# A sliding-window attention layer on one core: a new order of the seven products over three named banks, slots of their own for small tasks, softmax by groups with the sink as a 129th column

## The chip, the core and the metric

The kernel runs on one of the eight cores of a Trainium2 chip. The metric is device time in microseconds, from the program's start to its end. Three runs of the kernel before took 1522.75 to 1527.77 us, with a median of 1525.52. A further execution was taken with the hardware profiler; all busy times, waits and durations below are from that one.

The engines are TensorE (PE; its weight loads are PEld), VectorE (DVE), ScalarE (ACT), GpSimd (POOL) and SyncE (SP), which here only issues DMAs. TensorE writes to PSUM, which has eight banks of 128 x 512 float32.

## The reference

One decoder layer, of a width of 1024, on 4096 tokens: RMSNorm, a combined projection to queries, keys, values and a gate, attention over a window of 128 keys with a T5 bias and a learned sink per head, the gate, the output projection, the residual and a last RMSNorm.

```python
def swa_sink_mixer(xn, w_in, sinks, w_out, t5_table):
    q, k, v, z = jnp.split(xn @ w_in, [nq, nq + nkv, nq + 2 * nkv], axis=-1)
    o = banded_attention(q_heads(q, B, T), kv_heads(k, B, T), kv_heads(v, B, T),
                         t5_table, SWA_WINDOW, sinks)
    return (merge_heads(o, B, T) * jax.nn.silu(z)) @ w_out
...
    s = jnp.where(valid, s + bias[None, :, :, None], NEG)
    sk = jnp.broadcast_to(sinks.astype(jnp.float32).reshape(1, G, R, 1, 1, 1), s.shape[:-1] + (1,))
    p = jax.nn.softmax(jnp.concatenate([s, sk], axis=-1), axis=-1)[..., :-1]
    o = jnp.einsum('bgrnqk,bgnkd->bgrnqd', p.astype(v.dtype), vb)
...
    x = x + y.astype(x.dtype)
    return rms_norm(x, final_g)
```

There are 16 heads of 64 and 4 key-value heads. The sink takes part in the softmax's sum and then falls away.

## The kernel before

The tokens are worked on in 16 blocks of 256 (`tb`). Every float32 operand is held as two float16 halves, high and low, and each matmul is done as three passes (`PASSES`): high by high, high by low, low by high. ScalarE writes the high half and VectorE the low half (a subtraction), which is what the many "split" steps do.

The three large projections (q, z and the output o) are 1024 x 1024 matrices. From the third or fourth block on each is computed by Strassen's scheme in Winograd's form: both sides are cut into 2 x 2 pieces, seven products are formed from pieces and from sums of pieces (`s1`..`s4` on one side, `t1`..`t4` on the other), and the results are added. The first blocks use the plain eight products (`PLAIN`). The sums of the weights are prepared once, during blocks 1 to 3 (`sums`, four steps a matrix); the sums of the activations are made in each block: `x_sum` (GpSimd, in place in the tile `xf`, then the split `xs`) and `split_y` (GpSimd, in place in the tiles `y`, then the split `yo`).

For q and z a product is 48 matmuls of 128 x 128 x 128 (`product_t`, L307); for o it is 12 matmuls of 128 x 128 x 512 (`product_o`, L576). The seven products accumulate in three PSUM banks, which `ORDER` calls X, Z and W: X takes four of them, Z two, W one. After each product its bank is copied (`copy_m`, L336), added (`add_m`, L341; `add_mm` on GpSimd, L346) or passed on. The tag `pj` has three buffers for these banks and for those of the keys and values.

Six of the seven weight pieces of q stay in SBUF (`wq`); the seventh, and all pieces of z and o, are streamed from DRAM, 1 MB each, through a ring of three buffers `ws` (`load_s`, L286). SyncE issues these loads, and in the same queue those of `x` in two layouts (`load_x`: `xin` by rows, L99, and `xf` transposed, L102), of the residual `r` (L554), and the stores (L607). The `xf` halves have one buffer each, so a new half is loaded when the old one's last sum is split.

Attention is done in four pairs a block (a group pair `gp` and a half `t` of the block), each with two groups `e`:

- `scores` (L459): four tiles `s`, one for each of `e` and `r`, in a ring of two banks.
- `post` (L469 to L478): VectorE joins two parts of the score tile and writes score plus bias to the tile `c` (8 rows of 128 columns) with the row's maximum as an accumulated result.
- `exps` (L484 to L494): for all eight rows of the pair VectorE takes the larger of the maximum and the sink, scales it by -1/SCORE (`nm`) and forms the sink's difference (`dd`); ScalarE computes eight exponentials with their sums and one for the sink.
- `normalise` (L499 to L504): VectorE adds the two sums and takes the reciprocal; ScalarE multiplies all eight rows.
- `turn` (L512 to L518): four transposes a group, then the split `pt` and its masked copy `pm`.
- `values` and `gate` (L536, L543): the value products, and `y` = result times the gate `z`.

The order comes from a list of slots, 25 a block. Tasks are entered by `at` into one of four lists of a slot (`first`, `before`, `main`, `after`) and are emitted slot by slot. Block `tb`'s keys and values are in its slots 7 to 10, z in 11 to 17, the pairs from 11 to 39, and its output products in 43 to 49, which are slots 18 to 24 of the next block. A task such as `x_sum` or `split_y` does everything in its one slot: GpSimd's sum, ScalarE's half and VectorE's half. After emission a scheduler orders each engine's instructions by this priority and by when operands are ready, so an engine's order is near to the emitted one but not the same.

## Time and profile before

| | us |
|---|---|
| median of three runs | 1525.52 |
| profiled execution | 1529.2 |
| its span, from the first to the last instruction | 1527.3 |
| 11 steady block periods (430.5 to 1406) | 975.5 |
| mean granted TensorE clock over the span | 0.968 |

Busy time counts the union of an engine's instructions. The granted clock is the share of full speed that TensorE was given; in this trace it is either 1.0 or 0.5 at any moment, so a mean of 0.98 in a stretch means that 4% of it ran at half speed. In the rows of groups, "busy, mean ns" are the group's busy time in us and the mean duration of one instruction; where instructions of a group overlap, busy time over count is less than that mean. "x12" is a count. "[3.03 <-DMA ws<-wost]" is idle time of the engine just before the row, and what ended it.

Over the whole program the queue of SyncE moved 319 GB/s in the first 60 us and 225 GB/s from 430.5 to 1406.

### The profile page before, as it was taken

How to read it: one execution, taken by the hardware profiler on the slowest of the kernel's cores; microseconds unless marked ns; L12 is line 12 of the kernel's file. 1: busy time of each engine (PE TensorE's matmuls, PEld its weight loads, DVE VectorE, ACT ScalarE, POOL GpSimd, SP SyncE). 2: the span in 40 equal slices, each digit the busy share in tenths (PEclk: the TensorE clock that was granted, in tenths of full speed). 3: DMA queues.
4: the chain of work that ended last, by engine and by line, in shares of the span. 5: the costliest groups of instructions: out<-in, count | busy, mean ns of one | idle time of the engine just before them, and what ended most of it. 6: DMA issues, size and time to landing. Idle time of an engine off the chain costs nothing.

```text
span 1527.3 us, 39610 instructions
## 1 busy us (share of the span) xinstructions
PE 1398.7 (92%) x16234; PEld 1096.6 (72%) x16234; DVE 1060.1 (69%) x2783; ACT 955.9 (63%) x2633; POOL 389.1 (25%) x338
## 2 busy tenths in 40 slices
PE   5988899688999998999999898999989899999996
PEld 5987578367587785958778595877859587785952
DVE  8478766848848576776857677685767758676684
ACT  7367676645755676566567556656755665675672
POOL 0002423226204122131413213141321314132133
PEclk9999999799999999999999999999999999999998
DMA  9965654776967657475765747476574757656384
GB/s 367 289 223 173 263 214 179 248 272 254 342 225 252 246 197 280 157 280 166 262 238 201 278 155 276 167 266 238 205 256 160 271 183 251 235 205 251 122 301 185
DMA packets 70662, 356.24 MB, mean 233 GB/s; under 512 B 8752, under 2 KB 10832, under 8 KB 40656
## 3 DMA queue, kind: packets, MB, share of 16 engines
q1 hardware_dynamic: 61952, 336.92, 61.3%
q10 hardware_dynamic: 8528, 16.78, 3.0%
q8 instruction: 127, 2.08, 0.5%
q14 instruction: 55, 0.45, 0.1%
HBM read 318.03 MB, written 35.65 MB: 232 GB/s over the span
## 4 chain that ended last, share of the span: by engine, by line
PE 39%; DVE 27%; ACT 18%; DMA 9%; issue 4%; POOL 2%; SPq 0%; ACTq 0%; POOLq 0%; DVEq 0%
PE pj L307 21%; PE pj L576 11%; ACT c L492 7%; ACT c L504 5%; DVE xs L271 4%; DMA ws<-wost 3%; DVE q L355 3%; DVE pm L518 3%; DVE c L478 2%; PE tp L512 2%; DVE xb L259 2%; DVE pt L515 2%; PE o L536 2%; DVE z L405 2%; DVE xf L251 2%
## 5 line engine op out<-in xcount | busy, mean ns | idle before, releaser
L576 PE MATMUL pj<-ws,yo 128*128 128x512 f16 x1380 | 339.0, 398 | 42.3 <-DMA ws<-wost 14.5
L307 PEld LDWEIGHTS <-ws 128*128 128x128 f16 x6192 | 358.2, 99 | 15.2 <-issue 10.5
L307 PEld LDWEIGHTS <-wq 128*128 128x128 f16 x4800 | 280.4, 99 | 21.9 <-issue 11.8
L492 ACT ACTIVATE c<-c,nm 128x128 f32<-128x128 f32 x512 | 198.1, 388 | 148.0 <-DVE nm L486 146.7
L576 PEld LDWEIGHTS <-yo 128*128 128x128 f16 x1380 | 135.5, 102 | 209.8 <-issue 44.3
L307 PE MATMUL pj<-xb,ws 128*128 128x128 f16 x3024 | 184.0, 223 | 5.3 <-DMA ws<-wzs 3.5
L307 PE MATMUL pj<-xs,ws 128*128 128x128 f16 x3168 | 187.5, 219 | 1.3 <-ACT mc L336 1.3
L307 PE MATMUL pj<-xb,wq 128*128 128x128 f16 x2784 | 179.5, 222 | 8.4 <-ACT xb L258 3.5
L504 ACT ACTIVATE c<-c,rl 128x128 f32<-128x128 f32 x512 | 156.3, 388 | 3.7 <-DVE rl L501 3.7
L336 ACT ACTIVATE mc<-pj 128x512 f32<-128x512 f32 x160 | 93.8, 587 | 90.6 <-PE pj L307 76.3
L459 PE MATMUL s<-K,q 128*128 128x192 f16 x1024 | 111.5, 249 | 17.7 <-DVE m L478 12.4
L515 DVE SCALAR_TENSOR_TENSOR pt<-tp,pt 128x512 f16<-128x512 f32 x128 | 86.5, 680 | 52.8 <-ACT pt L514 52.5
L307 PE MATMUL pj<-xs,wq 128*128 128x128 f16 x2016 | 119.7, 219 | 0.0
L591 POOL TENSOR_TENSOR r<-r,mc 128x512 f32<-128x512 f32 x52 | 70.5, 1366 | 187.1 <-ACT mc L336 185.8
L478 DVE CUSTOM_DVE_ANT_0 c<-s,bias 128x128 f32<-128x128 f32 x496 | 116.1, 282 | 2.5 <-PE tp L512 1.6
L459 PEld LDWEIGHTS <-q 128*128 128x128 f16 x1024 | 84.2, 99 | 36.3 <-DVE m L478 19.0
L268 POOL TENSOR_TENSOR xf<-xf 128x512 f32<-128x512 f32 x56 | 78.3, 1400 | 101.1 <-DVE xb L259 78.1
L518 DVE TENSOR_TENSOR pm<-pt,own_m 128x1024 f16<-128x1024 f16 x128 | 101.5, 796 | 1.4
L514 ACT ACTIVATE pt<-tp 128x512 f16<-128x512 f32 x128 | 74.5, 587 | 42.4 <-PE tp L512 42.0
L156 POOL TENSOR_TENSOR wst<-wst 128x512 f32<-128x512 f32 x48 | 70.0, 1468 | 110.6 <-ACT wst L191 60.5
L326 PE MATMUL pj<-xb,wkv 128*128 128x256 f16 x768 | 92.7, 275 | 4.0 <-ACT xb L258 3.3
L492 ACT ACTIVATION_READ_ACCUMULATOR c<-c,nm 128x1 f32 x512 | 95.7, 187 | 0.0
(98 smaller groups left out, 2098.4 us busy)
## 6 DMA issues: line engine op xcount, KB each, us to landing
ws<-wos SPq DMA_DIRECT2D x63, 1024.0 KB, 6.4
ws<-wzss SPq DMA_DIRECT2D x52, 1024.0 KB, 5.7
ws<-wost SPq DMA_DIRECT2D x52, 1024.0 KB, 5.8
ws<-wzs SPq DMA_DIRECT2D x47, 1024.0 KB, 4.9
xin<-in_x SPq DMA_DIRECT2D x32, 512.0 KB, 5.8
xf<-in_xt SPq DMA_DIRECT2D x32, 512.0 KB, 6.2
r<-in_x SPq DMA_DIRECT2D x32, 512.0 KB, 4.3
out<-r SPq DMA_DIRECT2D x32, 512.0 KB, 5.7
```

The costliest lines, as they stand in the source:

```text
L268: nc.gpsimd.tensor_tensor(s, b[l], b[r], op=OP.subtract)
L307: nc.tensor.matmul(place(p, c), left(kc, wi)[:, c * P:(c + 1) * P], right_x(tb, right, kc, xi), start=fresh and c == 0 and k == 0, stop=c ...
L326: nc.tensor.matmul(p[:, gp * TB:(gp + 1) * TB], wkv[:, kc, wi, gp * P:(gp + 1) * P], xx(tb, xi, kc), start=k == 0, stop=k == 23)
L336: nc.scalar.activation(m, p, AF.Copy, scale=scale)
L459: nc.tensor.matmul(s[:, hp, 0:3 * HD], lhs, rhs, start=hl == 0, stop=hl == 1)
L478: nc.vector.tensor_tensor_reduce(out=cu, in0=sv, in1=b, scale=1.0, scalar=-3e38, op0=OP.add, op1=OP.max, accum_out=self.m[:, u:u + 1])
L492: nc.scalar.activation(cu, cu, AF.Exp, bias=nm[:, u:u + 1], scale=1.0 / SCORE, accum_out=l[:, u:u + 1])
L504: nc.scalar.activation(cu, cu, AF.Copy, scale=rl[:, u:u + 1])
L514: nc.scalar.activation(w[:, 0], p, AF.Copy, scale=SP)
L515: nc.vector.scalar_tensor_tensor(w[:, 1], p, SP, w[:, 0], op0=OP.mult, op1=OP.subtract)
L518: nc.vector.tensor_tensor(self.pm[e].rearrange("p l (h q) -> p (l h) q", h=4), w.rearrange("p l (h q) -> p (l h) q", h=4), own_m[:, None, ...
L576: nc.tensor.matmul(p, YO[left][:, yi, c * P:(c + 1) * P], right(c, wi), start=fresh and k == 0, stop=k == 11, skip_group_check=not fresh)
```

## The change

The matmuls are the same. What changes:

- **Order of the seven products.** Products are no longer in consecutive slots. In a block's output projection they are at slots 43, 44, 46, 48, 49, 47, 52: the sixth (the second on bank Z) comes ahead of the fourth and fifth, and slots between them are left to z and to the next q. The three banks have names of their own, `pa`, `pb`, `pc`, one buffer each, and each chain is told which of them is its X, Z and W.
- **Small tasks in slots of their own.** What a step did in one slot is cut up: `x_sum` (GpSimd) and `x_sum_split`; `sum_y` and `split_y`; `evac_v`, `diff_v` and `split_dv`; `evac_k` by halves; `x_norm` into `x_square` and `x_factor`; GpSimd's additions after a bank's copy. A slot now has eight lists (`PHASES`), and a table (`STEADY`, with `FIRST` and `LAST` for the ends) gives each task its slot. The steps of the weight sums are at slots 13, 17, 21 and 25, not 10, 13, 16 and 19.
- **Softmax.** The score tile `c` has a 129th column that GpSimd fills with the sink. `post` writes the negated, scaled score and reduces by minimum, starting from the sink, so that its accumulated result is the bias of the exponential; the sink's exponential is the 129th column's and is in the row's sum. `exps` and `normalise` are done for a group of four rows at a time. Of the four, ScalarE multiplies two and VectorE two.

```diff
     def x_sum(tb, n):
...
-        s = b[dst]
-        nc.gpsimd.tensor_tensor(s, b[l], b[r], op=OP.subtract)
+        dst, l, r = (x_blk(tb, *b) for b in SUM[n])
+        nc.gpsimd.tensor_tensor(dst, l, r, op=OP.subtract)
+
+    def x_sum_split(tb, n):
+        s = x_blk(tb, *SUM[n][0])
...
+        def post(self, e):
+            g = 2 * self.gp + e
+            if not self.c:
+                self.c = atile([P, 8, P + 1], F32, "c", 2)
...
+                nc.gpsimd.tensor_copy(self.c[:, :, P], sk)
...
-                nc.vector.tensor_tensor_reduce(out=cu, in0=sv, in1=b, scale=1.0, scalar=-3e38, op0=OP.add,
-                                               op1=OP.max, accum_out=self.m[:, u:u + 1])
+                    nc.vector.tensor_tensor_reduce(out=cu, in0=sv, in1=b, scale=-1.0 / SCORE,
+                                                   scalar=sink[:, g, r, hp:hp + 1], op0=OP.add, op1=OP.min,
+                                                   accum_out=self.m[:, u:u + 1])
...
-            nc.vector.tensor_tensor(mx, self.m, sk, op=OP.max)
-            nc.vector.tensor_scalar(nm, mx, -1.0 / SCORE, None, op0=OP.mult)
-            nc.vector.tensor_tensor(dd, sk, mx, op=OP.subtract)
...
+        def exps(self, e):
+            for u in range(4 * e, 4 * e + 4):
+                cu = self.c[:, u, :]
+                nc.scalar.activation(cu, cu, AF.Exp, bias=self.m[:, u:u + 1], scale=-1.0,
+                                     accum_out=self.l[:, u:u + 1])
+
+        def normalise(self, e):
+            rl = work.tile([P, 4], F32, tag="rl", name="rl", bufs=3)
+            nc.vector.reciprocal(rl, self.l[:, 4 * e:4 * e + 4])
+            for u in range(4):
+                cu = self.c[:, 4 * e + u, :P]
+                if u % 2:
+                    nc.scalar.activation(cu, cu, AF.Copy, scale=rl[:, u:u + 1])
+                else:
+                    nc.vector.tensor_scalar(cu, cu, rl[:, u:u + 1], None, op0=OP.mult)
...
+    PHASES = ("bank", "attn", "sum", "split", "soft", "load", "main", "scores")
+    work_of = [{n: [] for n in PHASES} for _ in range(total)]
+
+    def bank(key, name):
+        banks[key] = ps(f"p{name}")
+        return banks[key]
...
-    PLAN = {"q": range(0, 7), "k": 7, "v": 9, "z": range(11, 18), "pairs": (11, 17, 23, 29), "out": range(43, 50)}
+    STEADY = {
+        "q": (0, 1, 3, 5, 6, 4, 9), "k": (7, 8), "v": (10, 12), "z": (11, 13, 14, 15, 17, 16, 20),
+        "o": (43, 44, 46, 48, 49, 47, 52),
...
+        "ysum": {"s1": 40, "s2": 43, "s4": 44, "s3": 46},
+        "ysplit": {"11": 40, "s1": 41, "12": 43, "s2": 44, "s4": 45, "s3": 47, "22": 49},
...
+        "xsum": {"t1": 17, "t2": 23, "t3": 25, "t4": 26}, "xsumsplit": {"t1": 22, "t2": 24, "t3": 26, "t4": 28},
+    }
...
-        at(before, SLOTS + (10, 13, 16, 19)[c], sums, w_q, c, True, sum_q)
+        at("soft", SLOTS + (13, 17, 21, 25)[c], sums, w_q, c, True, sum_q)
```

Two places show how the order moves, both in a steady block, where the output products of one block run beside the sums of x for the next. First SyncE's queue there before; `wos` and `wost` are weights of o, `wzs` and `wzss` of z, and the numbers are buffers:

```order
L286 DMA ws_10062<-wzs22_90 128x4096
L286 DMA ws_10163<-wos11_102 128x4096
L286 DMA ws_10219<-wost1_98 128x4096
L286 DMA ws_10292<-wost2_104 128x4096
L102 DMA xf_11133<-in_xt 128x1024
L286 DMA ws_10357<-wos21_105 128x4096
L102 DMA xf_11135<-in_xt 128x1024
L286 DMA ws_10444<-wost3_103 128x4096
L286 DMA ws_10478<-wos22_99 128x4096
L286 DMA ws_10537<-wost4_101 128x4096
```

And the same queue in the changed kernel, where L302 is `load_s`, L105 `load_xf` and L99 `load_xin`:

```order
L302 DMA ws_11357<-wos11_102 128x4096
L99 DMA xin_16557<-in_x 128x1024
L302 DMA ws_11420<-wost1_98 128x4096
L99 DMA xin_16557<-in_x 128x1024
L302 DMA ws_11482<-wzs22_96 128x4096
L302 DMA ws_11543<-wost2_103 128x4096
L105 DMA xf_12228<-in_xt 128x1024
L302 DMA ws_11619<-wos22_104 128x4096
L302 DMA ws_11646<-wos21_105 128x4096
L105 DMA xf_12230<-in_xt 128x1024
L302 DMA ws_11684<-wost3_100 128x4096
L302 DMA ws_11827<-wost4_99 128x4096
```

The last z weight has moved in among the weights of o, `wos22` ahead of `wos21`, and one more weight stands between the two `xf` loads; the second `xf` load is still just ahead of `wost3`.

Second, VectorE's queue. Before, from the split of the second `xf` half (`xb`) to the split of its last sum (`xs`), and what follows:

```order
L259 TENSOR_TENSOR xb_11923<-xf_11135,xb_11923 128x4x256
L405 SCALAR_TENSOR_TENSOR z_11835<-z_11835,cc_11833 128x512
L515 SCALAR_TENSOR_TENSOR pt0_11901<-tp_11896,pt0_11901 128x512
L405 SCALAR_TENSOR_TENSOR z_11772<-z_11772,cc_11770 128x512
L515 SCALAR_TENSOR_TENSOR pt1_11944<-tp_11939,pt1_11944 128x512
L405 SCALAR_TENSOR_TENSOR z_11920<-z_11920,pj_11405 128x512
L518 TENSOR_TENSOR pm0_11904<-pt0_11901,own_m_110 128x1024
L271 TENSOR_TENSOR xs_12099<-xf_11135,xs_12099 128x4x128
L469 COPY_PREDICATED s_11974<-sel_115,s_11974 128x2x64
L518 TENSOR_TENSOR pm1_11947<-pt1_11944,own_m_110 128x1024
```

In the changed kernel the end of that way, from the last score reduction of the next softmax (`ISA`, on `c`) to the same split (`xs` from `xf_10786`, L287):

```order
L515 ISA m_11813 128x1
L528 RECIPROCAL rl_11863<-l_11607 128x4
L528 RECIPROCAL rl_11971<-l_11607 128x4
L430 SCALAR_TENSOR_TENSOR z_11744<-z_11744,pb_11137 128x512
L534 TENSOR_SCALAR c_11605<-c_11605,rl_11863 128x128 x2
L534 TENSOR_SCALAR c_11605<-c_11605,rl_11971 128x128
L573 SCALAR_TENSOR_TENSOR y00_11893<-o_11843,z_11535 128x512
L534 TENSOR_SCALAR c_11605<-c_11605,rl_11971 128x128
L287 TENSOR_TENSOR xs_12077<-xf_10786,xs_12077 128x4x128
L506 COPY_PREDICATED s_11806<-sel_115,s_11806 128x2x64
```

Before, six operations stand between `xb` and that `xs`. In the changed kernel `xb` (not shown) is 44 rows ahead of it: score reductions, two other splits of sums, `yo`, `pt`, `pm` and the four normalisations come in between.

More of the change, by code (lines that the diff above doesn't have):

```diff
@@ L634, in go, with chain @@
+    def chain(slots, key, names, f, steps):
         def go(n):
-            b = ORDER[n][1]
-            if n in (0, 1, 3):
-                banks[key, b] = ps("pj", 3)
-            f(n, banks[key, b])
+            b = "XZW".index(ORDER[n][1])
+            p = bank((key, b), names[b]) if n in (0, 1, 3) else banks[key, b]
+            f(n, p)
         for n, s in enumerate(slots):
-            at(main, s, go, n)
-            at(before, s + 1, lambda n=n: steps[n](banks[key, ORDER[n][1]]))
-    def chain_t(slots, tb, key, left, place, done):
+            at("main", s, go, n)
+            at("bank", s + 1, lambda n=n: steps[n](banks[key, "XZW".index(ORDER[n][1])]))
@@ L662, in go @@
                 if k == 1:
-                    banks[key, b] = ps("pj", 3)
+                    bank((key, b), names[b])
                 f(i, j, k, banks[key, b], k == 1)
             for k in (1, 2):
-                at(main, slots[2 * b + k - 1], go, k)
-            at(before, slots[2 * b + 1] + 1, lambda b=b, i=i, j=j: done(i - 1, j - 1, banks[key, b]))
-    def plain_t(slots, tb, key, left, place, done):
-        plain(slots, (key, tb),
+                at("main", slots[2 * b + k - 1], go, k)
@@ L671, in plain_t @@
+            at("bank", slots[2 * b + 1] + 1, lambda b=b, i=i, j=j: done(i - 1, j - 1, banks[key, b]))
+    def plain_t(slots, tb, key, names, left, place, done):
+        plain(slots, (key, tb), names,
               lambda i, j, k, p, fresh: product_t(tb, left(f"{i}{k}"), f"{k}{j}", p, place, fresh),
               lambda gp, t, p: done(tb, gp, t, p))
[L675 to L676 removed]
@@ L711, in tile_swa_block @@
-            at(first, s + 10, pr.values)
-            at(first, s + 10, pr.gate)
-        out0 = s0 + plan["out"][0]
-        slots = range(out0, out0 + 7)
-        if tb < PLAIN["o"]:
-            for n, b in enumerate(("11", "21", "12", "22") * 2):
-                at(before, out0 + n - 3, load_s, ("o", n), b, wos[b])
-            for b, s in zip(BLOCKS, (-2, -1, 2, 3)):
-                at(before, out0 + s, split_y, tb, b)
-            plain(slots, ("o", tb),
+            for e, (sc, po, ex, no, tu) in enumerate(((sc0, po0, ex0, no0, tu0), (sc1, po1, ex1, no1, tu1))):
+                at("scores", sc, pr.scores, e)
+                at("attn", po, pr.post, e)
+                at("soft", ex, pr.exps, e)
+                at("soft", no, pr.normalise, e)
+                at("attn", tu, pr.turn, e)
@@ L721, in tile_swa_block @@
+            at("attn", va, pr.values)
+            at("attn", ga, pr.gate)
+        if isplain["o"]:
+            slots = S["oplain"]
+            for n, (b, s) in enumerate(zip(("11", "21", "12", "22") * 2, slots)):
+                at("load", s - 4, load_s, ("o", n), b, wos[b])
+            for b, s in S["yplain"].items():
+                at("split", s, split_y, tb, b)
+            plain(slots, ("o", tb), "cbac" if tb + 1 < PLAIN["z"] else "cabc",
                   lambda i, j, k, p, fresh: product_o(f"{i}{k}", stream(("o", 4 * i + 2 * j + k - 7), f"{k}{j}"), p,
@@ L732, in tile_swa_block @@
-            chain(slots, ("o", tb),
-                  lambda n, p: product_o(LEFT[n], stream("o", RIGHT[n]), p, n in (0, 1, 3)), steps)
-        at(before, out0 - 3, load_r, tb)
+            for n, s in enumerate(S["o"]):
+                at("load", s - 4, load_s, "o", RIGHT[n], wos[RIGHT[n]])
+            for n, s in S["ysum"].items():
+                at("sum", s, sum_y, tb, n)
+            for n, s in S["ysplit"].items():
+                at("split", s, split_y, tb, n)
+            keep = {}
@@ L751, in tile_swa_block @@
+            if tb + 1 >= min(PLAIN["q"], PLAIN["z"]):
+                for n in SUM:
+                    at("sum", S["xsum"][n], x_sum, tb + 1, n)
+                    at("split", S["xsumsplit"][n], x_sum_split, tb + 1, n)
+    for tb in range(NTB):
+        block(tb)
     for t in range(2):
-        x_norm(0, t)
+        x_square(0, t)
+    x_factor(0)
     x_row(0)
```

326 lines of the change are left out of this document (165 added, 161 removed), and 8 rows, old and new, of the table STEADY.

## The prediction

> **What bounds the kernel now.** I read the busy line of the page first, then the stretches, then the timeline of TensorE in one block, the DMA issues of SyncE, and the chain of waits. The busy line says which engine to watch:
>
> ```profile
> PE 1398.7 (92%) x16234; PEld 1096.6 (72%) x16234; DVE 1060.1 (69%) x2783; ACT 955.9 (63%) x2633; POOL 389.1 (25%) x338
> ```
>
> TensorE works for 1398.7 of 1527.3 us, and the change leaves its matmuls as they are: the same 128x128 products, scores, transposes and value products, in another order. So time can only come out of TensorE's idle time and out of time that it works at half clock. The stretches tell where those are (columns: length, then busy time of PE, PEld, DVE, ACT and POOL, then the granted clock and the share of DMA):
>
> ```profile
> 60.00:430.50 370.50, 319.74 (x3595) 248.82 (x3592) 265.43 (x692) 235.69 (x641) 103.35 (x80) 0.94 0.69 250
> 430.50:1406.00 975.50, 927.51 (x11002) 732.88 (x10999) 677.03 (x1808) 610.79 (x1717) 253.34 (x221) 0.98 0.63 225
> 1406.00:1527.30 121.30, 107.04 (x1042) 73.98 (x1040) 74.39 (x207) 69.95 (x214) 28.20 (x24) 0.95 0.55 204
> 695.60:785.10 89.50, 84.51 (x999) 66.50 (x999) 62.04 (x167) 56.32 (x161) 22.86 (x20) 0.98 0.64 226
> 1231.90:1318.20 86.30, 82.70 (x1001) 66.13 (x1000) 61.28 (x165) 55.51 (x159) 22.94 (x20) 1.00 0.66 234
> ```
>
> After the ramp (to 60, not shown) come the early blocks, which also prepare weights (to 430.5), 11 steady blocks, and the end. A steady block takes 975.5 / 11 = 88.7 us, with (975.5 - 927.5) / 11 = 4.4 us of TensorE idle. The last two rows are one block each, with the same 1000 matmuls: at full clock TensorE works 82.7 us on it, at a mean of 0.98 about 84.4. So what a steady block can give at most is 4.4 + (927.5 / 11 - 82.7) = 4.4 + 1.6 = 6.0 us, 66 us in all 11. Where it is lost, TensorE's timeline of one block shows (start, length, and in brackets the idle time before and what ended it):
>
> ```profile
> 757.63 0.40 PE L536 MATMUL o<-pm,dv 128*64 128x512 f16 x1
> 758.78 0.81 PE L536 MATMUL o<-pm,dv 128*64 128x512 f16 x5 [0.74 <-DVE pm L518]
> 760.34 0.93 PE L459 MATMUL s<-K,q 128*128 128x192 f16 x8 [0.75 <-DVE m L478]
> 761.43 2.75 PE L576 MATMUL pj<-ws,yo 128*128 128x512 f16 x12 [0.16 <-DMA ws<-wos]
> 764.01 0.82 PE L459 MATMUL s<-K,q 128*128 128x192 f16 x8
> 767.87 4.44 PE L576 MATMUL pj<-ws,yo 128*128 128x512 f16 x12 [3.03 <-DMA ws<-wost]
> ```
>
> Two waits of 0.75 us for VectorE and one of 3.03 us for a streamed weight. The product after that wait takes 4.44 us in place of 2.75: the half clock. SyncE's issues of the same stretch (the second row of weights, `ws<-wost`, is the one waited for):
>
> ```profile
> 753.66 0.38 SPq L286 DMA_DIRECT2D ws<-wos  x1
> 757.96 0.33 SPq L102 DMA_DIRECT2D xf<-in_xt  x1
> 758.38 0.38 SPq L286 DMA_DIRECT2D ws<-wost  x1
> ```
>
> And the chain of waits, followed back from the late product:
>
> ```profile
> 754.96 1.30 DVE pm L518
> 756.25 1.67 DVE xs L271
> 757.93 0.22 DVE s L469
> 758.15 0.14 SPq L102
> ...
> 758.38 9.35 DMA ws<-wost
> ```
>
> SyncE issues in order. The load of the next `xf` half waits until VectorE has split the last sum of the old one (`xs`, done at 757.9), and the weight queued behind it goes out at 758.4 and lands 9.35 us later. So the weight wait is itself a VectorE wait: the bound beside TensorE is VectorE's queue in the part of a block where the output products run.
>
> **The change part by part, in a steady block.** *Output products among other products.* TensorE now has a z product and parts of two q products between the seven output products. I count what lies between the last `xs` split and the product of the late weight (`wost3`) in the two orders. Before, TensorE has one output product, scores and values left when the split is done at 757.9, 4.6 us of work without the waits. In the new order the split stands where two output products (2 x 2.6), six of the value matmuls (0.7), scores (0.7) and 17 matmuls of a q product (1.0) are still ahead of it: 7.6 us. The page's landing time for these weights is the median of this row, and the worst here is the 9.35 us above:
>
> ```profile
> ws<-wost SPq DMA_DIRECT2D x52, 1024.0 KB, 5.8
> ```
>
> 7.6 against 5.8: I put the weight wait at nothing, with a bound of 9.35 - 7.6 = 1.8 us a block. With the 3 us gap gone the half clock should go too: the block 1231.9 to 1318.2 above kept full clock although TensorE waited there before the same product, only for 1.78 us:
>
> ```profile
> 1302.66 2.75 PE L576 MATMUL pj<-ws,yo 128*128 128x512 f16 x12 [1.78 <-ACT c L504]
> ```
>
> *VectorE's queue.* From the split of the first sum (`xs_11786`) to the last of the four normalisations of the next softmax (`c_11605`), the new order has on VectorE 3 sum splits, 1 `xb`, 3 gates `z` (2 from `cc`, 1 from a bank), 5 predicated copies, 10 score reductions, 2 `yo`, 2 `pt`, 2 `pm`, 1 K copy, 2 reciprocals, 4 normalisations and 1 `y`. What each costs:
>
> ```profile
> L478 DVE CUSTOM_DVE_ANT_0 c<-s,bias 128x128 f32<-128x128 f32 x344 | 80.2, 282 | 0.5
> L518 DVE TENSOR_TENSOR pm<-pt,own_m 128x1024 f16<-128x1024 f16 x86 | 66.7, 776 | 1.1
> L570 DVE TENSOR_TENSOR yo<-y,yo 128x512 f16<-128x512 f32 x78 | 60.2, 771 | 7.6 <-ACT yo L569 6.3
> L515 DVE SCALAR_TENSOR_TENSOR pt<-tp,pt 128x512 f16<-128x512 f32 x86 | 58.4, 679 | 48.9 <-ACT pt L514 48.8
> L271 DVE TENSOR_TENSOR xs<-xf,xs 128x512 f16<-128x512 f32 x44 | 58.2, 1323 | 15.8 <-ACT xs L270 15.8
> L469 DVE COPY_PREDICATED s<-sel,s 128x128 f32<-128x128 int32 x172 | 45.6, 286 | 4.1 <-PE s L459 3.4
> L259 DVE TENSOR_TENSOR xb<-xf,xb 128x1024 f16<-128x1024 f32 x22 | 36.3, 1649 | 0.0
> L405 DVE SCALAR_TENSOR_TENSOR z<-z,cc 128x512 f32<-128x512 f32 x33 | 27.6, 837 | 0.0
> L486 DVE TENSOR_SCALAR nm<-mx 128x8 f32<-128x8 f32 x43 | 7.2, 168 | 1.1
> L476 DVE TENSOR_TENSOR c<-s,bias 128x128 f32<-128x128 f32 x16 | 3.9, 282 | 0.1
> ```
>
> By busy time over count (they overlap a little): 3 x 1.32 + 1.65 + 2 x 0.84 + 0.67 + 5 x 0.265 + 10 x 0.233 + 2 x 0.77 + 2 x 0.68 + 2 x 0.78 + 0.4 + 2 x 0.2 + 4 x 0.2 + 0.69 = 18.4 us. (The z gate from a bank, `y`, the K copy and the reciprocals are estimates by their neighbours: 0.67 and 0.69 like `pt`, 0.4 for half of `pm`, 0.2 like `nm`.) VectorE starts that list when TensorE has 1.2 us left of a z product, since two operations (0.69 and 0.84) stand between. From there to the transposes that need the four normalised pieces TensorE has, beside those 1.2 us, three output products (2.6 each, 761.43 to 764.01 above), one z product, 28 score matmuls, 8 transposes and 12 value matmuls (0.40 and 0.81 for 6 above). The other lengths are in the chain of waits of another block:
>
> ```profile
> 1318.25 8.15 PE pj L307 x144
> 1326.40 0.66 PE s L459 x8
> 1327.06 0.44 PE tp L512 x4
> ```
>
> Three products take 8.15, so 2.7 each, eight score matmuls 0.66 and four transposes 0.44: 1.2 + 7.8 + 2.7 + 2.3 + 0.9 + 1.2 = 16.1 us. VectorE is 2.3 us longer, so **TensorE waits 2.3 us a block**, at the scores whose two banks VectorE must clear and at the value products.
>
> *What I priced by bounds.* A normalisation on VectorE (128x128, SBUF to SBUF) isn't in the trace: it lies between 0.168 (`nm`, 128x8) and 0.282 us (`c` at L476, 128x128 from a bank), and I take 0.2, near the smaller, as those rows overlap to 0.24 and 0.17. The reduction now takes its start value from `sink`, a column in place of a constant. It may cost nothing, and at most what a column adds elsewhere:
>
> ```profile
> L131 DVE SCALAR_TENSOR_TENSOR wq<-wst,gs,wq 128x512 f16<-128x512 f32 x16 | 11.0, 742 | 0.1
> L131 DVE SCALAR_TENSOR_TENSOR wsp<-r,wsp 128x512 f16<-128x512 f32 x16 | 10.5, 687 | 9.7 <-ACT wsp L130 9.5
> ```
>
> That is 742 - 687 = 55 ns, for 10 of them 0.55 us; I take half, 0.3. With 0.2 for small waits elsewhere (`tp` after `xf` stands at 0.2 now) a steady block loses 2.3 + 0.3 + 0.2 = 2.8 us, not 6.0: **3.2 us x 11 = 35 us**.
>
> *Edits at nothing.* The removed maximum, scale, difference and sum of the softmax (4 small VectorE operations and one ScalarE exponential a pair) and half of the normalisations leave ScalarE, which had 88.7 - 55.5 = 33 us idle a block; the 129th column adds one element in 129. The sink copies (4 a block) are added to GpSimd, which is busy 23 us of 86. If these lost that cover, the exponentials would wait for one GpSimd operation a pair (1.37 us, the row under rival 2). Named banks: each bank is copied while TensorE runs another product (2.6 us against 0.6 us), as now.
>
> *Early blocks.* Idle 370.5 - 319.7 = 51 us, and half clock on top. Of the waits there the change touches two:
>
> ```profile
> PE tp L512 <- ACT c L504: 6.9, 5, 4.4
> PE s L459 <- ACT K L367: 4.4, 2, 3.3
> ```
>
> The normalisation is halved and done by groups, and K is cleared one half at a time. I take these 11 us, and 1 for the clock after them: 12. The weight sums move to slots three to six later, which can hide more or push other work back: the bounds are 35 and -10. *The end* keeps its last product, norm and store; the reordered output products may save 3 of its 14 us of idle time (0 to 8).
>
> **Sum.** 35 + 12 + 3 = 50 us off the profiled execution's own 1529.2 us (span 1527.3) gives 1479. That execution was 3.7 us above the median of the runs, 1525.5, so I predict **1475 us**.
>
> **A rule of the Trainium skill against this.** In the rows above `xs` (L271) takes 1323 ns and `yo` (L570), of the same shape, 771. The Trainium skill, "SBUF — State Buffer", section "Who interferes with whom", says why such a gap can be: GpSimd and VectorE share a port pair that one instruction locks for its whole length, and `tensor_scalar` in a two-port mode is one of the operations that takes it. The trace agrees for `xs`, and cannot show it for the new normalisation. By that rule each normalisation would wait half a GpSimd operation in the 26% of the time that GpSimd is busy, an estimate of 0.18 us each: 6 of them lie in the crowded stretch or just ahead of it, 1.1 us a block, and the sum would be 1487.
>
> **Rivals.** (1) *VectorE takes the whole place of the late weight.* The chain above already ends on VectorE, and the new order still has an `xf` load waiting for VectorE ahead of `wost3`. If a block keeps its 6.0 us, only 12 + 3 remain: 1525.5 - 15 = 1510. For it: 18.4 us of VectorE work against 16.1. Against it: two output products and more as cover, in place of one. (2) *Slower: the normalisations on VectorE block on GpSimd.* If each of the six in the crowded stretch waits as long as a GpSimd operation
>
> ```profile
> L268 POOL TENSOR_TENSOR xf<-xf 128x512 f32<-128x512 f32 x44 | 60.1, 1365 | 93.1 <-DVE xb L259 75.8 <-DVE xs L271 16.5
> ```
>
> that is 6 x 1.37 = 8.2 us on the engine that TensorE waits for, 8.2 - 3.2 = 5.0 us a block lost, 55 us in 11 blocks, less 15: 1525.5 + 40 = 1566. It decides from 3.2 / 6 = 0.53 us each. For it: `xs` loses 0.55 us to something of that kind. Against it: `yo` and `pm` lie at 0.77 and do not show it. (3) *All waits go.* VectorE's stretch gets by with the slack ahead of it: 66 + 20 us, 1440. (4) *Gains and losses cancel,* the steady gain being given back by the weight sums in the early blocks: near 1525.
>
> **How the numbers follow.** Forecast 0.62, rival (1) 0.14, (2) 0.09, (3) 0.09, (4) 0.06. A measurement of this kernel tells about 0.3% from no change. Faster by more than that: the forecast, (1) and (3), 0.85; same 0.06; slower 0.09. The range holds the forecast with its bounds (steady 66 to 17 us, early 35 to -10) and reaches to rivals (1) and (3): 1438 to 1512, leaving out (2) and (4).
>
> **What would show it.** In the profile after, a steady block should last 85 to 86 us (82.7 + 2.8), with no wait of TensorE for a weight above 1 us and the clock at 1.00 there. TensorE's waits should stand at the scores and value products, behind VectorE's reductions and `pt`. VectorE should be busy all through the stretch before the transposes. A steady block near 88 with half clock means rival (1); normalisations of over 0.5 us on VectorE mean rival (2); what the early blocks take shows the second term. I would be wrong from the ground up if TensorE's busy time a block moved from 82.7, since then its matmuls are not the same work.

## The result, and the profile after

Four runs of the changed kernel took 1444.52 to 1452.32 us, with a median of 1450.95; the kernel before, beside them, 1524.67. The ratio is 0.950, with a 95% interval of 0.947 to 0.953: 74 us faster, where 50 were forecast. The profiled execution took 1452.32 us, with a span of 1450.2. Its busy line, to be held against that of before:

```profile
PE 1362.3 (94%) x16234; PEld 1084.9 (75%) x16234; DVE 1121.3 (77%) x2847; ACT 882.0 (61%) x2313; POOL 436.4 (30%) x402
```

VectorE has become busier (1060.1 to 1121.3) and ScalarE less so (955.9 to 882.0). TensorE, with the same 16234 matmuls, is busy for 36 us less; the rest of the gain is its idle time. The stretches of both kernels, with the prediction's columns, are cut at the same mark: 60 us, the first product of the keys of block 4, that of block 15, and the end. Before:

```profile
60.00:443.70 383.70, 332.94 (x3831) 262.02 (x3828) 269.76 (x700) 242.20 (x653) 105.75 (x84) 0.94 0.69 250
443.70:1421.60 977.90, 929.91 (x11029) 735.25 (x11026) 681.68 (x1823) 614.56 (x1734) 252.22 (x219) 0.98 0.62 223
1421.60:1527.30 105.70, 91.44 (x778) 58.40 (x776) 65.41 (x185) 59.67 (x183) 26.93 (x23) 0.94 0.60 220
```

After, and below it one steady block and, in that block, the stretch in which VectorE is crowded:

```profile
60.00:405.90 345.90, 315.08 (x3822) 253.56 (x3822) 269.30 (x695) 213.95 (x551) 108.59 (x95) 0.97 0.73 264
405.90:1342.60 936.70, 908.84 (x10981) 731.10 (x10980) 739.26 (x1896) 573.77 (x1553) 294.87 (x266) 1.00 0.65 237
1342.60:1450.20 107.60, 94.93 (x830) 60.81 (x827) 71.09 (x181) 52.77 (x144) 28.85 (x28) 0.95 0.59 216
836.80:921.10 84.30, 82.52 (x1000) 66.17 (x998) 67.75 (x171) 51.55 (x141) 26.28 (x24) 1.00 0.64 238
872.00:889.60 17.60, 15.82 (x130) 9.53 (x127) 17.28 (x48) 11.80 (x38) 9.51 (x6) 1.00 0.90 352
```

The early blocks gave 37.8 us, the 11 steady blocks 41.2, and the end lost 1.9. About 50 matmuls have moved from the steady part over the last mark (one q product, 2.7 us), so like for like the steady part gave 38.5 and the end 0.8. The forecast was 12, 35 and 3. The steady block shown takes 84.3 us (84.5 is the median of the 11), with 1.8 us of TensorE idle. What is left of waits in that block (engine, line, releaser: us in total, times, longest):

```profile
PE s L488 <- DVE m L515: 1.3, 1, 1.3
PE o L566 <- DVE pt L545: 0.3, 1, 0.3
PE pc L607 <- DMA ws<-wos: 0.2, 1, 0.2
```

That is one of the better blocks. Over the 11 periods TensorE was idle for 48.0 us before and is for 27.9 us now, 2.5 us a block. The largest waits in them, before:

```profile
PE pj L576 <- DMA ws<-wost: 13.4, 5, 3.0
PE pj L576 <- ACT c L504: 13.4, 5, 3.5
```

and after:

```profile
PE s L488 <- DVE m L515: 10.5, 8, 2.7
PE pb L323 <- DMA ws<-wzss: 6.0, 3, 2.1
PE pa L607 <- DMA ws<-wos: 3.0, 2, 1.6
PE o L566 <- DVE pt L545: 2.1, 5, 0.9
PE pc L607 <- DMA ws<-wost: 2.0, 2, 1.3
```

Both rows of before are the late weight: in the five blocks whose wait is put down to an exponential (`ACT c`), a `wost` load landed 0.13 to 0.14 us before the product started. So ten of the 11 blocks waited for it, 26.8 us in all. After, all waits for weights together are 13.2 us, and those behind VectorE 12.6.

And TensorE's timeline in the block shown, from the split of the last sum on:

```profile
889.62 0.49 PE L488 MATMUL s<-K,q 128*128 128x192 f16 x4
889.96 1.04 PE L542 MATMUL tp<-ident,c 128*128 128x128 f32 x8
890.83 2.75 PE L607 MATMUL pa<-ws,yo 128*128 128x512 f16 x12
893.42 0.82 PE L488 MATMUL s<-K,q 128*128 128x192 f16 x8
894.08 2.75 PE L607 MATMUL pb<-ws,yo 128*128 128x512 f16 x12
896.76 0.84 PE L566 MATMUL o<-pt,v 128*64 128x512 f16 x6
897.53 1.12 PE L323 MATMUL pa<-xb,wq 128*128 128x128 f16 x17
898.49 2.75 PE L607 MATMUL pc<-ws,yo 128*128 128x512 f16 x12
```

SyncE in the same stretch:

```profile
890.18 0.33 SPq L105 DMA_DIRECT2D xf<-in_xt  x1
890.61 3.32 SPq L302 DMA_DIRECT2D ws<-wost  x2
```

The `xf` load still stands right ahead of `wost3`, as in the order shown above. But its product starts at 898.49, 7.9 us after the issue, with two products, scores, values and 17 q matmuls before it: no brackets, no wait, and each product lasts 2.75. The four groups that the prediction had priced (busy us, mean ns):

```profile
L515 DVE CUSTOM_DVE_ANT_0 c<-s,bias,sink 128x128 f32<-128x128 f32 x496 | 146.8, 343 | 1.4
L534 DVE TENSOR_SCALAR c<-c,rl 128x128 f32<-128x128 f32 x256 | 86.7, 387 | 2.1
L287 DVE TENSOR_TENSOR xs<-xf,xs 128x512 f16<-128x512 f32 x56 | 47.5, 850 | 0.2 <-ACT xs L286 0.2
L281 POOL TENSOR_TENSOR xf<-xf 128x512 f32<-128x512 f32 x56 | 97.0, 1742 | 62.9 <-DVE xs L287 31.5 <-DVE xb L269 30.9
```

### The profile page after: what moved, and what is told of

Its sections match the earlier page's. It is cut to its first block, busy times and chain, and to the rows that moved or that the text cites. A ratio compares the mean times of both kernels' runs of the same rounds, so it can differ in the third digit from the quotient of the medians.

```text
span 1450.2 us, 39444 instructions
## 1 busy us (share of the span) xinstructions
PE 1362.3 (94%) x16234; PEld 1084.9 (75%) x16234; DVE 1121.3 (77%) x2847; ACT 882.0 (61%) x2313; POOL 436.4 (30%) x402
## 4 chain that ended last, share of the span: by engine, by line
PE 46%; DVE 23%; DMA 13%; issue 8%; ACT 6%; POOL 2%; SPq 0%; ACTq 0%; POOLq 0%; DVEq 0%
PE pa L323 9%; PE pb L323 8%; PE pc L607 6%; PE pb L342 4%; PE o L566 4%; PE pc L390 3%; PE pa L607 3%; PE s L488 3%; PE pc L323 2%; DVE yo L601 2%; PE tp L542 2%; DVE c L515 2%; DVE xf L261 2%; DMA ws<-wost 2%; PE pb L607 2%
## 5 line engine op out<-in xcount | busy, mean ns | idle before, releaser
L323 PEld LDWEIGHTS <-wq 128*128 128x128 f16 x4800 | 273.2, 98 | 21.7 <-issue 11.2
L523 ACT ACTIVATE c<-c,m 128x129 f32<-128x129 f32 x512 | 199.9, 392 | 118.6 <-DVE m L515 118.1
L607 PE MATMUL pc<-ws,yo 128*128 128x512 f16 x768 | 181.7, 387 | 14.1 <-DMA ws<-wos 9.1
L515 DVE CUSTOM_DVE_ANT_0 c<-s,bias,sink 128x128 f32<-128x128 f32 x496 | 146.8, 343 | 1.4
L323 PE MATMUL pb<-xs,ws 128*128 128x128 f16 x1872 | 112.7, 221 | 8.0 <-DMA ws<-wzss 7.6
L545 DVE SCALAR_TENSOR_TENSOR pt<-tp,pt 128x512 f16<-128x512 f32 x128 | 85.5, 684 | 41.5 <-ACT pt L544 41.0
L281 POOL TENSOR_TENSOR xf<-xf 128x512 f32<-128x512 f32 x56 | 97.0, 1742 | 62.9 <-DVE xs L287 31.5
L601 DVE TENSOR_TENSOR yo<-y,yo 128x512 f16<-128x512 f32 x103 | 86.0, 837 | 33.3 <-ACT yo L600 32.9
L594 POOL TENSOR_TENSOR y<-y,y 128x512 f32<-128x512 f32 x52 | 70.1, 1347 | 105.0 <-DVE y L573 93.8
L532 ACT ACTIVATE c<-c,rl 128x128 f32<-128x128 f32 x256 | 84.9, 391 | 18.8 <-DVE rl L528 18.8
L523 ACT ACTIVATION_READ_ACCUMULATOR c<-c,m 128x1 f32 x512 | 96.3, 188 | 0.0
L506 DVE COPY_PREDICATED s<-sel,s 128x128 f32<-128x128 int32 x256 | 68.9, 286 | 34.9 <-PE s L488 34.0
L607 PE MATMUL pa<-ws,yo 128*128 128x512 f16 x384 | 90.9, 384 | 5.2 <-DMA ws<-wos 3.0
```

The costliest lines, as they stand in the source:

```text
L281: nc.gpsimd.tensor_tensor(dst, l, r, op=OP.subtract)
L323: nc.tensor.matmul(place(p, c), left(kc, wi)[:, c * P:(c + 1) * P], right_x(tb, right, kc, xi), start=fresh and c == 0 and k == 0, stop=c ...
L515: nc.vector.tensor_tensor_reduce(out=cu, in0=sv, in1=b, scale=-1.0 / SCORE, scalar=sink[:, g, r, hp:hp + 1], op0=OP.add, op1=OP.min, accum ...
L523: nc.scalar.activation(cu, cu, AF.Exp, bias=self.m[:, u:u + 1], scale=-1.0, accum_out=self.l[:, u:u + 1])
L532: nc.scalar.activation(cu, cu, AF.Copy, scale=rl[:, u:u + 1])
L545: nc.vector.scalar_tensor_tensor(w[:, 1], p, SP, w[:, 0], op0=OP.mult, op1=OP.subtract)
```

## The experiments

Twelve kernels, run in four groups. In the table, "early" is 60 us to the keys of block 4 and "block" the median of the 11 steady periods, both from the one profiled execution, which can lie up to 10 us from the median (a_order_old: 1467.70 against 1477.26); "ratio" is to the kernel before.

| kernel | median us | ratio, 95% interval | early | block |
|---|---|---|---|---|
| before | 1524.67 | | 383.7 | 88.8 |
| after | 1450.95 | 0.947 to 0.953 | 345.9 | 84.5 |
| a_sums_old | 1451.55 | 0.949 to 0.957 | 358.2 | 84.3 |
| a_order_old | 1477.26 | 0.963 to 0.972 | 349.3 | 85.8 |
| a_soft_old | 1472.36 | 0.961 to 0.969 | 346.2 | 85.5 |
| a_fused | 1454.48 | 0.950 to 0.957 | 351.0 | 84.7 |
| a_tasks_old | 1446.61 | 0.942 to 0.953 | 350.3 | 83.9 |
| t_only | 1483.67 | 0.965 to 0.977 | 350.5 | 86.5 |
| t_ring | 1464.65 | 0.956 to 0.962 | 343.2 | 85.6 |
| t_pairs_old | 1473.90 | 0.963 to 0.970 | 340.1 | 85.4 |
| t_sums_tasks | 1516.17 | 0.991 to 0.997 | 370.8 | 88.5 |
| a_norm_act | 1437.20 | 0.936 to 0.947 | 334.3 | 84.5 |
| a_const | 1436.79 | 0.936 to 0.946 | 341.0 | 83.7 |
| a_best | 1441.81 | 0.942 to 0.948 | 346.6 | 84.3 |

### One part undone on the changed kernel

```diff
a_sums_old
-        at("soft", SLOTS + (13, 17, 21, 25)[c], sums, w_q, c, True, sum_q)
+        at("soft", SLOTS + (10, 13, 16, 19)[c], sums, w_q, c, True, sum_q)
...
a_order_old
-        "q": (0, 1, 3, 5, 6, 4, 9), ... "z": (11, 13, 14, 15, 17, 16, 20),
-        "o": (43, 44, 46, 48, 49, 47, 52),
+        "q": (0, 1, 2, 3, 4, 5, 6), ... "z": (11, 12, 13, 14, 15, 16, 17),
+        "o": (43, 44, 45, 46, 47, 48, 49),
```

> The changed kernel with the four steps of each weight sum back at slots 10, 13, 16 and 19. The early blocks gained about 35 us where I had forecast 12. Theory A (the new slots of the sums give what I missed): about 23 us come back, 1474 us, all of it before block 4, and the steady block stays at 84.4. Theory B (order and softmax gave it, the slots of the sums are worth little): 1446 to 1457 us.

Theory B: 1451.55. The early stretch did lengthen by 12 us (358.2), but the block after it took 83.9 us in place of 90.3, since the last step of the output weights' sums had gone from it: the work had only changed its block.

> The changed kernel with the seven products of q, z and o in consecutive slots again (43 to 49 for o); all else stays. My theory (the spread products give the weights time and remove half clock): the wait for an o weight and the half clock come back, a steady block goes from 84.4 to 87.5 or 88, 11 blocks give 35 to 40 us and the time is about 1486 to 1490 us. Rival (the softmax and the tasks in slots of their own free VectorE, so that the order is worth little): no weight wait above 1 us, 1451 to 1460 us.

In between: 26 us. The block rose to 85.8, not to 88, and the wait for an o weight did not come back block by block; one block (836 to 922) has only

```profile
PE o L566 <- ACT pt L544: 1.2, 1, 1.2
PE s L488 <- DVE m L515: 0.2, 1, 0.2
```

So the consecutive products alone do not make the weight late, which is against my theory. Over the steady part this execution waits 28.0 us, as the changed kernel does (27.9); what rose is TensorE's busy time, by 11.2 us for the same work, of which 3.4 us more at half clock explain 1.7. The rest of that rise is open.

```diff
a_soft_old
-                    nc.vector.tensor_tensor_reduce(out=cu, in0=sv, in1=b, scale=-1.0 / SCORE,
-                                                   scalar=sink[:, g, r, hp:hp + 1], op0=OP.add, op1=OP.min,
...
+                nc.vector.tensor_tensor_reduce(out=cu, in0=sv, in1=b, scale=1.0, scalar=-3e38, op0=OP.add,
+                                               op1=OP.max, accum_out=self.m[:, u:u + 1])
...
+            ex, no = max(ex0, ex1), max(no0, no1)
+            at("soft", ex, pr.exps)
+            at("soft", no, pr.normalise)
...
a_fused
-    "xsumsplit": {"t1": 22, "t2": 24, "t3": 26, "t4": 28},
+    "xsumsplit": {"t1": 17, "t2": 23, "t3": 25, "t4": 26},
```

> The changed kernel with the softmax of before: maximum, sink apart, by pairs, all eight normalisations on ScalarE; transposes at the earliest one slot after the normalisation. My theory (the softmax gives only the waits behind the normalisation in the early blocks, 11 us, and costs VectorE time in the steady ones): 1452 to 1463 us, a steady block of 83.5 to 84.5. Rival (the softmax carries a large part of the gain in the steady blocks too, by a shorter chain from scores to transposes): a steady block of 86 or more with TensorE waiting at the transposes, 1475 us or more.

Nearly the rival: 1472.36. The early stretch, where I had seen the whole worth of the softmax, did not move (346.2); the block rose to 85.5 with 14.5 us of waits at the transposes behind ScalarE's normalisation in the steady part (6 waits), against none in the changed kernel. I had expected the block to get shorter.

> The changed kernel with each sum of x and of y split in the slot of its GpSimd sum, as before, order and softmax as changed. Theory A (VectorE, in order, stands behind GpSimd's sum of 1.4 to 1.7 us at three places of the crowded stretch): up to 3 us a steady block, 33 us, 1480 us, with waits at scores behind VectorE. Theory B (the scheduler puts other VectorE work between sum and split anyway): within 5 us of 1451.

Theory B (the y splits were put back with those of x). Single parts so far: 26 + 21 + 3 + 1, 51 of the 74 us, and none had brought the early stretch back above 358.

```diff
a_tasks_old (with a_fused)
-    "qp22": 12, "qs11": 7, "qs12": 12, "qs22": 13, "vd": 14, "dv": 19,
+    "qp22": 7, "qs11": 6, "qs12": 5, "qs22": 7, "vd": 13, "dv": 13,
-    "op": (49, 47, 52, 53), "on": (53, 55), "om": (54, 57), ...
+    "op": (44, 45, 47, 50), "on": (53, 55), "om": (53, 55), ...
-    nc.scalar.activation(xin[tb, t], xin[tb, t], AF.Square, accum_out=sq[tb, t])
+    nc.scalar.activation(junk, xin[tb, t], AF.Square, accum_out=sq[tb, t])
```

> The changed kernel with all the small tasks together again (sums of x and y with their splits, both halves of K, the value difference with its split, the squares of a block with their factor and in a buffer of the ring op, GpSimd's additions at the copy of the bank); order and softmax as changed. The undone order gave 26 us, the undone softmax 21, sums and splits 3, the slots of the weight sums 0: 50 of 74. Theory A (the other small tasks carry the rest, in the early blocks, which no undone part has slowed yet): 1470 to 1478 us, the early stretch (60 us to the keys of block 4) 365 us or more in place of 346. Theory B (each part alone is enough there, so that undoing one shows nothing): 1451 to 1460 us, the early stretch below 355.

Below both: 1446.61, within the spread of the changed kernel's own runs. On top of the new order and softmax the small tasks' slots are worth nothing.

### Several parts undone together

t_only joins the edits of a_order_old and a_soft_old. To it, t_ring adds one edit and t_pairs_old another; t_sums_tasks joins t_pairs_old, a_sums_old and a_tasks_old (with the slots of done tasks moved to those of the consecutive products).

```diff
t_ring
-        banks[key] = ps(f"p{name}")
+        banks[key] = ps("pj", 3)
t_pairs_old
-        for (gp, t), (sc0, po0, ...) in S["pairs"].items():
+        for (gp, t), s in zip(((0, 0), (1, 0), (0, 1), (1, 1)), starts):
...
t_sums_tasks
-    "xq": (11, 12), "xm": 13,
+    "xq": (9, 9), "xm": 9,
```

> Order and softmax both undone, so that the small tasks in slots of their own and the named banks stay alone of the change. If the parts add, 1451 + 26 + 21 = 1498 us, which leaves 27 us to the small tasks. If they cover the same waits (theory B): both together lose more than one by one, 1510 to 1525 us, with the early stretch back at 370 us or more.

1483.67: 33 us for both, less than the 47 of the two alone, and the early stretch stays at 350.5. Neither statement holds; 41 us remained that no run had touched.

> As t_only (order and softmax undone, 1484 us), and the four pairs of a block back at the slots of before, with scores tile by tile and everything up to the value products in the old sequence. 41 us of the 74 are left in t_only and neither the small tasks nor the slots of the weight sums hold them. Theory A (the pairs' slots hold them): 1510 to 1525 us, the early stretch at 365 us or more in place of 350, and the wait for a weight behind VectorE's split back in the steady blocks. Theory B (the named banks hold them): 1480 to 1490 us, early stretch at 350.

> As t_only (1484 us), with the three banks in one ring of three buffers again in place of three names. Theory A (pair slots): 1480 to 1490 us. Theory B (banks): 1510 us or more, with TensorE waiting at products for the copy of a bank by ScalarE in the early blocks. In consecutive slots the ring hands the banks out in the order in which the names do, up to where q and o change places, so I expect A here.

Both came out faster than t_only, by 10 and 19 us, and outside what either theory said: neither the pairs' slots nor the banks' names hold the 41 us. They also warn: I expected nothing of the ring, and it moved the time by 19 us, some 10 of them in one period (block 4's, 100.3 to 90.1 us). Each edit lets the scheduler order the engines anew; even in a_const (below), whose edit is one operand of a VectorE instruction, scores stand elsewhere among TensorE's products than in the changed kernel. That the new order alone makes the 19 us is not shown, as the ring also hands the banks out in turn and not by name. But differences up to about 20 us cannot be put down to the edited part by the time alone, and the 26 and 21 us of the single parts are not much more.

> As t_pairs_old (order, softmax and pair slots undone, 1474 us), with the small tasks together and the slots of the weight sums undone as well; the squares of a block at slot 9. Named banks and the slots of the other small tasks (the steps of x, the loads, the values' second half, the end of a block) stay. Each of the two was worth nothing when undone alone on the changed kernel. Theory A (each hides the other's loss): 1500 to 1525 us, the early stretch at 365 us or more in place of 340. Theory B (neither holds the early gain, it lies in the slots that stay changed): 1470 to 1480 us, the early stretch below 352.

The numbers of theory A: 1516.17, 42 us slower than t_pairs_old, the early stretch at 370.8 and the block at 88.5, and no t-kernel was near that before. Whether both of the two are needed for it was not run. What is different in a steady block (TensorE's timeline, t_sums_tasks):

```profile
744.04 0.38 PE L566 MATMUL o<-pm,dv 128*64 128x512 f16 x1 [1.15 <-DVE pm L548]
746.31 0.81 PE L566 MATMUL o<-pm,dv 128*64 128x512 f16 x5 [1.90 <-DVE pm L548]
747.05 2.76 PE L607 MATMUL pb<-ws,yo 128*128 128x512 f16 x12
749.65 0.82 PE L489 MATMUL s<-K,q 128*128 128x192 f16 x8
752.92 2.75 PE L607 MATMUL pc<-ws,yo 128*128 128x512 f16 x12 [2.44 <-DMA ws<-wost]
```

and the chain of waits that ends there (start, length):

```profile
739.54 1.08 DVE z L431
740.63 1.68 DVE xs L288
742.30 1.68 DVE pm L548
743.99 0.60 DVE z L431
744.58 1.08 DVE xs L288
745.67 0.02 issue
745.68 0.02 SPq L105
...
746.15 6.63 DMA ws<-wost
```

This is the chain of the kernel before again: VectorE's split `xs`, the `xf` load waiting for it, the weight behind that load in SyncE's queue, 6.63 us of landing, and a product that waits 2.44 us. It stands in eight of the 11 blocks, 19.9 us in all (in three of them the wait is put down to an exponential, but the weight landed 0.13 us before the product). t_pairs_old, with the same consecutive products but the small tasks in slots of their own, has no wait for `wost` in its steady part. What differs is SyncE's queue there (the first row is `wost3`):

```profile
631.81 0.32 SPq L302 DMA_DIRECT2D ws<-wost  x1
634.72 1.31 SPq L105 DMA_DIRECT2D xf<-in_xt  x2
```

Both `xf` loads now stand behind `wost3`, in nine of the ten steady blocks that load an `xf`, so that weight no longer waits for VectorE's split. a_order_old has this order in seven of the ten, without a wait for `wost`; its two waits for it (2.4 and 1.1 us) fall in its last two, where an `xf` load stands ahead of `wost3` again. t_sums_tasks has one `xf` load ahead of it in all ten, and the kernel before has both. What t_pairs_old waits for, in 7 blocks and 10.5 us in all, is the first o weight, whose load goes out when a z product has freed its buffer: nothing of VectorE's.

### The price of the softmax on VectorE

```diff
a_norm_act
-                if u % 2:
-                    nc.scalar.activation(cu, cu, AF.Copy, scale=rl[:, u:u + 1])
-                else:
-                    nc.vector.tensor_scalar(cu, cu, rl[:, u:u + 1], None, op0=OP.mult)
+                nc.scalar.activation(cu, cu, AF.Copy, scale=rl[:, u:u + 1])
a_const
-                                                   scalar=sink[:, g, r, hp:hp + 1], op0=OP.add, op1=OP.min,
+                                                   scalar=3e38, op0=OP.add, op1=OP.min,
```

> The changed kernel with all four normalisations of a group on ScalarE. The eight a block pair on VectorE took 0.34 us of busy time each, 5.4 us a block, against the 0.2 that I forecast. Theory A (VectorE bounds the crowded stretch, as my sum has it): its four there are 1.4 us, the waits of TensorE at the scores (1.3 us a block) go, 83.2 us a block, 1437 to 1443 us. Theory B (the chain from exponential to transposes counts): four on ScalarE take 1.6 us in a row in place of 0.8, TensorE waits for them, 1455 to 1462 us.

> The changed kernel with the reductions started from a constant, so that the sink is left out of the bias of the exponential (it stays in the sum as the 129th column). The reductions should fall from 0.296 to about 0.234 us of busy time each, as before the change, 32 a block, 2.0 us, of which 10 lie in the crowded stretch. Theory A (VectorE bounds that stretch): 0.6 us of it comes off the wait at the scores, 7 us in 11 blocks, 1443 to 1446 us. Theory B (hidden): 1449 to 1453 us. If the reductions keep their 0.296, the column isn't what makes them longer.

> The changed kernel with both easings of VectorE: all normalisations on ScalarE and reductions from a constant (the sink is left out of the bias of the exponential and stays in the sum). Alone each took 14 us off 1451. If VectorE is the bound that both relieve and it is still one after each, they add to 1422 to 1426 us. If the first already freed what TensorE waited for, 1432 to 1437 us, and the waits left at the scores stay at about 0.9 us a block. The bound is TensorE's own work, 82.7 us a block.

Both single edits beat the changed kernel by 14 us. a_const took 0.8 us off the median block, near the 0.6 of theory A, but its time lies 6 us below what that theory said, and the place is not shown: in the steady part the wait at the scores fell only from 10.5 to 9.5 us, while the waits for weights fell from 13.2 to 4.6. Its row of the groups settles the price of the column:

```profile
L515 DVE CUSTOM_DVE_ANT_0 c<-s,bias 128x128 f32<-128x128 f32 x496 | 116.6, 282 | 1.3
```

282 ns as before the change, against 343. a_norm_act has the time of theory A but not its place: the block stayed at 84.5, with 1.6 us of waits at the scores in one block, and 12 of the 20 us by which its profiled execution is shorter came from the early stretch. Together the two do not add: a_best lies behind each of them and outside both statements, mostly by its early stretch (346.6). With 19 us from an edit that should do nothing, I cannot say that the two oppose each other. The best kernel measured is a_const or a_norm_act, at 1437 us.

## Why the prediction was right, and where not

**Bound and mechanism in a steady block: right, with two errors that cancel.** TensorE's work on a block's 1000 matmuls stayed at 82.5 to 82.7 us, and the half clock is nearly gone (by the clock's intervals in the traces, 37.5 us of the steady part before and 6.8 after). Idle time gave 20.1 of the 41.2 us (38.5 like for like) and busy time 21.1; the prediction has 1.6 us a block, 17.6, for each, 35 in all. VectorE's crowded stretch was to be 18.4 us against 16.1 of TensorE; the row of 872.0 to 889.6, from `xs` to the last normalisation, holds the same list and has VectorE busy for 17.28 of 17.6 us and TensorE for 15.82. A block loses 2.5 us in the mean (27.9 / 11), near the 2.8 forecast, but only half of it where it was forecast: behind VectorE it loses 1.1 us (12.6 / 11) and not 2.3, and to late weights, which I put at nothing, 1.2 (13.2 / 11). Over the 11 blocks seven waits for a weight are above the 1 us that I had named as the limit. That the sum came out so near is luck.

**The terms within it: one too cheap, one too dear, one right where it counts.** The column of the reduction costs 61 ns, above my bound of 55; I took half. A normalisation was put at 0.2 us, near the smaller row; the mean duration is 0.387 (0.34 by busy time over count, as the sum counts). The mean hides two kinds. Sorted by whether a GpSimd instruction overlapped it (worked out from the start and length of each in the trace):

| on VectorE | alone: count, mean ns | beside GpSimd: count, mean ns |
|---|---|---|
| normalisation, L534 | 203, 280 | 53, 794 |
| split `xs`, L287, after | 35, 679 | 21, 1136 |
| split `xs`, L271, before | 19, 681 | 37, 1525 |
| score reduction from PSUM, L515 | 372, 343 | 140, 342 |

One pair of rows shows it, VectorE's timeline and GpSimd's (start, length):

```profile
898.78 1.31 DVE L534 TENSOR_SCALAR c<-c,rl 128x128 f32<-128x128 f32 x1
```

```profile
898.74 1.27 POOL L622 TENSOR_TENSOR r<-r,mc 128x512 f32<-128x512 f32 x1 [2.31 <-DVE rl L528]
```

So rival 2 named a real mechanism: some normalisations wait for a whole GpSimd operation, 1.31 us. But it takes 53 of 256, and none of those in the crowded stretch: ahead of the late weight's load they last 0.27 to 0.29 us in all ten blocks, and as they overlap they start 0.2 us apart, the price that I took. In the mean a normalisation waits 0.107 us (387 - 280 ns), below the 0.53 from which the rival decides. The too dear term was `xs`: 850 ns against the 1323 that I took, as fewer of the splits run beside a GpSimd operation (21 of 56 in place of 37). The Trainium skill, "SBUF — State Buffer", section "Who interferes with whom", says that VectorE and GpSimd share one pair of ports, and that a VectorE instruction with at most one SBUF input, outside the two-port modes, does not meet GpSimd. The table agrees: the reduction, with one input in PSUM, takes the same time either way. The estimate that the prediction made by that page was 0.18 us for each normalisation, where 0.107 was measured.

Three smaller readings were off without moving the forecast. The 12 value matmuls stand at 1.2 us, which is what the rows shown give for 6; TensorE's work left after the split before is 5.2 us by those rows, not 4.6; and the lower bound of the steady term, 17, is 35 - 1.8 x 11 = 15 by the prediction's own bound of the weight wait.

**The late weight: right result, by a narrow margin, and not by that remedy alone.** I put its wait at nothing because the new order has 7.6 us of products in front of `wost3`, against 5.8 us of landing. The wait did go, from 26.8 to 2.0 us. But 5.8 is the median of all 52 such loads; this one took 7.8 to 9.5 us in the ten blocks before and takes 6.4 to 9.3 after, and in four of the ten its product starts within 0.06 us of the landing. Nor are the spread products needed for it: t_pairs_old has the consecutive order and no wait for `wost` in its steady blocks, a_order_old only two (3.5 us), and t_sums_tasks has it back in eight. The chain that I had read (VectorE, `xf` load, weight) is shown: with consecutive products the wait comes only in blocks where an `xf` load stands ahead of `wost3`. The small tasks in slots of their own break it by putting the `xf` loads behind that weight. In the changed kernel the `xf` load is still ahead, and the products hide the wait; a_tasks_old, with the small tasks together and the products spread, waits 2.8 us for `wost`. That the spread products do this without the new softmax was not run.

**The early blocks: the step that failed, by size.** I forecast 12 us from two waits (11) and the clock (1), with a bound of 35; it gave 37.8. About 12 of these only change stretch: with the weight sums at their old slots (a_sums_old) the early stretch is 358.2 and the steady part 926.5, the time the same. The two waits went from 11.3 to 1.6 us, so that part was right. What was mis-sized is the rest: TensorE's idle time fell by 19.9 us (383.7 - 332.9 to 345.9 - 315.1) and its busy time by 17.9 for nearly the same number of matmuls, of which the clock explains at most 12 (44.4 us at half clock before, 20.5 after). Nearly all of the gain lies in one period, from the keys of block 2 to those of block 3, before and after:

```profile
207.10:348.00 140.90, 118.41 (x1307) 90.59 (x1305) 92.62 (x219) 84.75 (x217) 45.22 (x37) 0.89 0.59 212
213.10:308.80 95.70, 88.41 (x1061) 70.11 (x1059) 71.19 (x166) 57.60 (x144) 31.94 (x27) 1.00 0.62 221
```

There TensorE was idle for 22.5 us and is for 7.3, and the clock went from 0.89 to 1.00; some of its matmuls now come in earlier or later periods. Of the 22.5 us the prediction's two waits are 4.7; the others, at the scores, for a z weight, for `pt` and for `yo`, it did not price. In a stretch with many waits of 2 to 4 us the half clock is a term, not an afterthought. Nor were the waits to be had one by one: order, softmax, sums or small tasks, undone alone, leave the stretch at 346 to 358; only sums and tasks undone with the rest bring 371.

**The end** gave 0.8 for 3. **Rivals 1 and 4** fall: the block left 88 far behind, and nothing was given back. The time is nearer to rival 3 (1440) than to the forecast, but 27.9 us of waits remain in the steady blocks; it is the early blocks that brought it there.

**What stays open:** which of the weight sums and the small tasks costs the 31 us in the early blocks of t_sums_tasks; the last 9 to 12 us between that kernel and the one before; about 6 us of the early busy time, and the busy time of a_order_old; and how much of each single number is reordering.

## What to carry to other kernels

Look for what a late transfer waits behind: in an in-order queue a load for another purpose, waiting for a slow engine, makes every load after it late, and that can be cured by the order of the queue or at the consumer. Parts of a change that cure the same wait are not additive; undoing one may show nothing, so undo them together before calling a part worthless. Where a scheduler orders the instructions, run an edit that should do nothing, to see what size of difference means anything (here one moved the time by 19 us of 1480). And list the waits of the whole stretch, not of one block: the block shown has no late weight, while over the 11 the weights cost as much as VectorE.

## What the runs showed of the hardware

- A column in place of a constant as the start of a reduction of 128x128 from PSUM costs VectorE 61 ns (282 to 343); taking it out again gave exactly 282.
- A VectorE operation from SBUF to SBUF of 0.28 us can take 1.31 us beside one on GpSimd, and GpSimd pays as well: its sums of x went from 1400 to 1742 ns in the mean, the operation being the same, and are at 1568 with the normalisations off VectorE (a_norm_act).
- The length of a wait does not decide on the half clock, its place does: in t_sums_tasks TensorE waited up to 3.20 us for a weight and kept the full clock for 809 us, while waits of 3.03 (before, at 764.8 us) and 2.06 (after, at 1121.4) were followed by 3.4 us of half clock. In each of the 14 traces the intervals of half clock start on one grid of 3.413 us and last one step of it or several, but for the last, which ends with the program. From 60 us on, 112 steps at full clock had TensorE busy for less than 40% of the step, and half clock followed all of them; 5323 had it busy for more than 60%, and half clock followed one; of the 149 between, 20. The wait of 3.03 us left TensorE 11% of its step and that of 2.06 us 39.5%; the one of 3.20 us fell into two steps, with 60 and 46% (worked out from the start and length of the matmuls and the clock's intervals). The Trainium skill, "TensorE: Matmul & The Clock Gate", section "What's actually happening", has a free-running window of about 3.4 us, and these traces agree.
